# Gate projections of branches A and D for two token groups: computed in the groups' first phase and stored, instead of beside the scan

## The chip, the core and the metric

The kernel runs on one core of one Trainium2 chip. The metric is the device time of one execution in microseconds (us), the median of several runs. Engines: PE is TensorE (matmuls; PEld is its loading of weights), DVE is VectorE, ACT is ScalarE, POOL is GpSimd, SP issues the DMAs. Each engine works through its own instructions in order and waits for others by semaphores.

## What is computed

One layer of a hybrid backbone over two sets of tokens (2048 latent tokens and 128 context tokens, 1024 channels). What matters here of the reference:

```
h = rmsnorm(x, norm_g) * (1 + scale[:, None]) + shift[:, None]
p = h @ w_in
qkv, g_a, beta_logit, a_logit, uv, g_b, x_c, g_c, x_d, g_d = jnp.split(p, _split_points(), axis=-1)
y_a, S_new = deltanet_branch(qkv, g_a, beta_logit, a_logit, S0, ...)   # short conv, chunked scan, both directions
y_b = sgu_branch(uv, g_b, ...)
y_c = pool_branch(x_c, g_c, pool_w, pool_scale)
y_d = fourier_branch(x_d, g_d, fourier_w)
out = jnp.concatenate([y_a, y_b, y_c, y_d], axis=-1) @ w_out
return x + gate[:, None] * out, S_new
```

Every branch ends in a product with `silu(g)` of its own gate columns, 256 columns of `p` each. `g_a` and `g_d` depend on `h` alone: they can be computed at any time at which `h` is in memory.

## The kernel before

The 2176 tokens are cut into three groups: 0 and 1 have 768 tokens each (12 chunks of 64), group 2 has 640, with the context tokens. The two operands of a projection are each held as a pair of fp32r parts (hi and lo) and multiplied in three matmuls (`mm3`, L250), over 8 slices of the channels: 24 matmuls for one tile of output in PSUM. `BIG` holds the group's normalized tokens `hT` for one group at a time, and beside it a ring of three slots for weights. `load_w` (L236 to L243) fetches a weight tile of 128 columns in two halves by SP, and splits it: hi by ACT (by DVE when `Ring.late` is set, after the first phase), lo by DVE for the first half and by POOL for the second. `proj_cm` runs such projections in chunks of tokens, into PSUM tiles `pj` of which there are three.

**The first phase**, `phase_a(gi)` for the groups 0, 1, 2 in turn: `x_fin` writes the group's `hT`; then come the columns of branch D and the decay inputs (`in_wxd`), branch C (`branch_c`), and for each of two pairs of heads K, then Q and V: `conv_proj` projects and evicts into `raw` (L813), `conv_post` makes the short convolution on DVE (`acc`, L830 and L832) and Silu (L834), squares Q and sums it (L843, L844), `k_tok`, `v_tok` and `pair_pre` write the scan's records to DRAM (`rec_d`, `com_d`). The tiles `acc` and `raw` have two buffers each; V's result stays in its `acc` until `v_tok` has read it. The triangular inverses of a group are solved in `lanes_solve` (L728, L730, a chain of steps shared by DVE and POOL) and written by `lanes_out` (L752 to L788): group 0's beside group 1's first phase, those of groups 1 and 2 together after it. Work of group 2's later projections (`r_store`, `r_gate`, `r_b`) runs beside that solve.

**The scan** (`scan`, L1043 to L1072) takes 34 steps, 2 for the context and 32 for the latent tokens, forward and backward at once. A step is a chain: matmuls with the state S, two operations on DVE (L1054, L1055), matmuls, a copy on ACT (`xn`, L1061), matmuls, and the new state on DVE (L1065). Its operands `R` and `C` are loaded by SP for each step (L1032, L1034), two steps deep. Between its steps PE runs the rest of the projections: for group 1 and then for group 0, `r_load` brings `hT` back from DRAM (`h_d`), `r_b` computes branch B, `r_gate(gi, 0)` the gate and product of branch C; `fourier` runs between r_b(1) and r_gate(1, 0). Gate A is `r_store(gi, 14, ga_d)`: projected in three chunks of 256 tokens, Silu, stored in DRAM. Gate D is `r_gate(gi, 1)`: projected the same way and multiplied at once with the stored result `raw_d`. For group 2 both were computed and stored (`ga_d`, `gd_d`) before the scan.

**The output** follows in 17 tiles of 128 tokens, the context first, then from the middle outwards (7, 8, 6, 9, ...): tile 7 and tile 8 need 18 steps of the latent scan, and each further pair two more. One tile is 96 matmuls of 256 columns (`yh`, `yl`), and its weights `wos` replace `hT` in `BIG`, so no output matmul can run before the last projection.

A scheduler orders each engine's instructions when the program is built: by priority, in the order of the code, where an instruction that isn't ready by its own account of time lets later ones pass. The engines then run that order.

## Time and profile before

| | us |
|---|---|
| median of 3 runs | 1256.94 |
| lowest, highest | 1252.34, 1257.28 |
| profiled execution, time | 1259.96 |
| profiled execution, span from first to last instruction | 1258.2 |
| granted TensorE clock, mean over the span | 0.917 |

The profile is of one execution. Its time is 1.8 us over its span and 3.0 us over the median. Busy time of an engine is the time in which it has an instruction under way; the granted clock is the share of full speed at which PE was allowed to run, and has two levels, 1.2 and 2.4 GHz, so a mean of 0.63 is a mixture of them. Times in the timelines are from the start of the span.

### The profile page before, as it was taken

The page shows a single profiled execution, that of the slowest core. Times are in us where ns is not written, and L with a number is a line of the kernel's source. Part 1 is how long each engine was busy: PE and PEld are TensorE (multiplying, and loading weights), DVE is VectorE, ACT ScalarE, POOL GpSimd, SP SyncE. Part 2 cuts the span into 40 slices and gives each one's busy share as a digit, 9 for nine tenths or more (in the row PEclk, how much of TensorE's full clock was granted, in tenths as well). Part 3 has the DMA queues.
Part 4 walks back from the last instruction along what each step waited for, and adds up shares of the span by engine and source line. Part 5 has one row for each costly group of instructions (what it writes and reads, how often), then busy time and mean ns, then how long its engine had stood idle before and what let it go on. Part 6 is the DMA issues. An engine that isn't in the chain of part 4 may idle for free.

```text
span 1258.2 us, 28860 instructions
## 1 busy us (share of the span) xinstructions
PE 1100.5 (87%) x11635; PEld 998.4 (79%) x11635; DVE 875.8 (70%) x1864; ACT 414.3 (33%) x836; POOL 560.2 (45%) x551
## 2 busy tenths in 40 slices
PE   5798999986578899878997989999899979999997
PEld 2598888875566889774886878888889969999997
DVE  3768886999987477999577263584433378888665
ACT  2355765444344585310523102112111211111111
POOL 1347456799973154797040033223132543432212
PEclk9999988998766899798998989999999969999999
DMA  9978559543271558425245656767735555544331
GB/s 303 331 265 269 148 136 254 189 102 72 60 169 40 128 129 188 111 82 189 61 122 164 168 149 180 232 211 253 208 119 177 176 169 164 174 144 140 122 126 68
DMA packets 251388, 204.21 MB, mean 162 GB/s; under 512 B 109138, under 2 KB 218706, under 8 KB 250998
## 3 DMA queue, kind: packets, MB, share of 16 engines
q1 hardware_dynamic: 251254, 202.37, 55.1%
q8 instruction: 91, 1.49, 0.5%
q14 instruction: 43, 0.35, 0.1%
HBM read 138.86 MB, written 63.46 MB: 161 GB/s over the span
## 4 chain that ended last, share of the span: by engine, by line
PE 35%; DVE 8%; DMA 7%; POOL 5%; issue 3%; SPq 2%; ACT 1%; DVEq 0%; POOLq 0%; ACTq 0%
PE pj L250 28%; DMA wst<-in_wt_dram 3%; PE pa L1043 3%; POOL LL L730 2%; POOL ltmp L728 2%; DVE BIG L240 1%; DMA tab<-in_cdft_dram 1%; DVE X L752 1%; POOL BIG L243 1%; PE pb L1384 1%; PE pc L1043 1%; SPq L1034 1%; DMA ga<-ga_d 1%; DMA wos<-in_wo_dram 1%; DVE BIG L1207 1%
## 5 line engine op out<-in xcount | busy, mean ns | idle before, releaser
L250 PE MATMUL pj<-BIG 128*128 128x256 f32 (+4 forms) x3888 | 638.6, 320 | 34.0 <-DVE BIG L240 7.8
L250 PEld LDWEIGHTS pj<-BIG 128*128 128x128 f32 x3888 | 581.2, 201 | 54.9 <-issue 13.9
L250 PE MATMUL pj<-BIG,yh 128*128 128x256 f32 x1088 | 196.9, 287 | 5.7 <-ACT BIG L1346 4.7
L250 PEld LDWEIGHTS pj<-BIG,yh 128*128 128x128 f32 x1088 | 164.8, 191 | 8.8 <-ACT BIG L1346 5.1
L243 POOL TENSOR_TENSOR BIG<-wst,BIG 128x512 fp32r<-128x512 f32 (+1 forms) x66 | 94.7, 1436 | 171.9 <-DVE BIG L240 77.7
L250 PE MATMUL pj<-BIG,yl 128*128 128x256 f32 x544 | 141.9, 286 | 0.0
L250 PEld LDWEIGHTS pj<-BIG,yl 128*128 128x128 f32 x544 | 99.0, 191 | 0.7
L240 DVE CAST BIG<-wst 128x512 fp32r<-128x512 f32 (+2 forms) x72 | 44.9, 624 | 75.9 <-DMA wst<-in_wt_dram 41.5
L1404 POOL TENSOR_TENSOR z<-z,xs 128x1024 f32<-128x1024 f32 x16 | 40.2, 2510 | 72.5 <-DVE z L1396 62.0
L832 DVE SCALAR_TENSOR_TENSOR acc<-raw,prm,acc 128x768 f32<-128x768 f32 (+1 forms) x72 | 68.6, 976 | 4.8 <-ACT acc L830 4.8
L1050 POOL TENSOR_TENSOR gS<-S,sc_s 128x256 f32<-128x256 f32 x32 | 21.5, 672 | 97.3 <-DVE S L1065 85.4
L728 POOL TENSOR_TENSOR ltmp<-LL 64x60 f32<-64x60 f32 (+29 forms) x60 | 60.9, 1015 | 5.4 <-ACT LL L717 2.0
L730 POOL TENSOR_TENSOR LL<-LL,ltmp 64x60 f32<-64x60 f32 (+29 forms) x60 | 61.8, 1031 | 3.3
L1365 ACT ACTIVATE yh<-yt 128x768 fp32r<-128x768 f32 (+1 forms) x34 | 20.6, 628 | 125.2 <-issue 59.9
L243 DVE TENSOR_TENSOR BIG<-wst,BIG 128x512 fp32r<-128x512 f32 (+1 forms) x66 | 52.7, 799 | 10.7 <-ACT BIG L242 8.4
L354 POOL TENSOR_TENSOR BIG<-h,BIG 128x384 fp32r<-128x384 f32 (+2 forms) x28 | 32.7, 1167 | 61.6 <-DVE BIG L353 57.8
L730 DVE TENSOR_TENSOR LL<-LL,ltmp 64x60 f32<-64x60 f32 (+29 forms) x60 | 53.8, 896 | 1.1
L242 ACT ACTIVATE BIG<-wst 128x512 fp32r<-128x512 f32 (+1 forms) x60 | 37.6, 633 | 51.1 <-DMA wst<-in_wt_dram 29.4
L728 DVE TENSOR_TENSOR ltmp<-LL 64x60 f32<-64x60 f32 (+29 forms) x60 | 53.2, 887 | 1.3
L1061 ACT ACTIVATE xn<-pa 128x256 f32<-128x256 f32 x34 | 13.0, 381 | 106.9 <-PE pa L1043 106.9
L1212 ACT ACTIVATE g<-pj 128x256 f32<-128x256 f32 (+1 forms) x64 | 22.6, 398 | 70.5 <-PE pj L250 61.3
L1396 DVE TENSOR_TENSOR z<-pj,gbc 128x256 f32<-128x256 f32 x68 | 26.1, 421 | 28.2 <-PE pj L250 27.9
(292 smaller groups left out, 1921.9 us busy)
## 6 DMA issues: line engine op xcount, KB each, us to landing
wst<-in_wt_dram SPq DMA_DIRECT2D x96, 256.0 KB
R<-rec_d SPq DMA_DIRECT2D x136, 128.0 KB
ada<-in_ada_dram SPq DMA_DIRECT2D x24, 512.0 KB
C<-com_d SPq DMA_DIRECT2D x68, 128.0 KB
xs<-xs_d SPq DMA_DIRECT2D x16, 512.0 KB
out_dram<-z SPq DMA_DIRECT2D x16, 512.0 KB
x<-in_xs_dram SPq DMA_DIRECT2D x13, 512.0 KB
xs_d<-x SPq DMA_DIRECT2D x13, 512.0 KB
```

What stands on the lines that cost most here:

```text
L240: nc.vector.tensor_copy(hi[:, ks, a:a + w], st[:, :, :w])
L242: nc.scalar.activation(hi[:, ks, a:a + w], st[:, :, :w], AF.Copy)
L243: (nc.vector if k0 == 0 else nc.gpsimd).tensor_tensor(lo[:, ks, a:a + w], st[:, :, :w], hi[:, ks, a:a + w].bitcast(F32), op=ALU.subtract)
L250: nc.tensor.matmul(out, lh[a](k), rh[b](k), start=(k == first and i == 0), stop=(k == last and i == 2))
L354: (nc.gpsimd if f % 2 else nc.vector).tensor_tensor(hT[1][:, f, off:off + w], h, hi.bitcast(F32), op=ALU.subtract)
L728: eng.tensor_tensor(tv, X[:, bs, j, j + 1:32].unsqueeze(2).to_broadcast([n, nb, j, ni]), bc(X[:, bs, 0:j, j], ni), op=ALU.mult)
L730: eng.tensor_tensor(X[:, bs, 0:j, j + 1:32], X[:, bs, 0:j, j + 1:32], tv, op=ALU.add)
L832: nc.vector.scalar_tensor_tensor(o, raw[:, si + j:si + j + n], w[:, j:j + 1], o, op0=ALU.mult, op1=ALU.add)
L1043: nc.tensor.matmul(ps[o, q], lh(q)[hp], rh[hp, q])
L1212: [lambda a, w, ps, t=t: nc.scalar.activation(t[:, a:a + w], ps[:, :w], func) for t in ts])
L1396: nc.vector.tensor_tensor(z[:, ns], ps, gbc[:, cd, ns], op=ALU.mult)
L1404: nc.gpsimd.tensor_tensor(z, z, xs, op=ALU.add)
```

## The change

For groups 0 and 1 a new function `early_gate` projects two gate tiles in the group's first phase, in two chunks of 384 tokens, behind Q and V of each pair: gate A (tiles 14, 15) in pair 0 and gate D (12, 13) in pair 1. The Silu goes into a tile of tag `acc`, the one that the convolutions use, and is stored in `ga_d` or `gd_d`. Beside the scan, `r_store` for groups 1 and 0 and `r_gate(gi, 1)` go away; the product of branch D is now made for all three groups in one loop at the end, with gate D loaded from `gd_d`.

```diff
+    def early_gate(gi, ct, dst):
+        for m in range(2):
+            t = cv_.tile([128, 784], F32, tag="acc", name="eg")
+            proj_cm([io["wt"][ct + m]], [(0, 384), (384, 384)],
+                    [lambda a, w, ps, t=t: nc.scalar.activation(t[:, a:a + w], ps[:, :w], AF.Silu)])
+            nc.sync.dma_start(out=dst[m, :, 768 * gi:768 * gi + 768], in_=t[:, :768])
+
     def conv_proj(g, cts, chunks):
...
             sv = conv_post(g, 3 * pair + 2, rv, ntok)
             pull()
+            if gi < 2:
+                early_gate(gi, 14 - 2 * pair, (ga_d, gd_d)[pair])
...
     r_gate(1, 0)
-    r_store(1, 14, ga_d)
-    r_gate(1, 1)
     f_es.close()
     op = [ctx.enter_context(tc.tile_pool(name="opa_", bufs=1, side="right", reuse_waits="tile"))]
     r_load(0)
     r_b(0)
     r_gate(0, 0)
-    r_gate(0, 1)
-    for m in range(2):
-        g = gt_(2)
-        nc.sync.dma_start(out=g, in_=gd_d[m, :, tks(2)])
-        r_mul(2, 1, m, g)
-    r_store(0, 14, ga_d)
+    for gi in (1, 2, 0):
+        for m in range(2):
+            g = gt_(gi)
+            nc.sync.dma_start(out=g, in_=gd_d[m, :, tks(gi)])
+            r_mul(gi, 1, m, g)
```

The built order shows the following. On ACT in group 0, behind the last eviction of V of pair 0 (acc_1266 is Q's buffer there, acc_1305 V's, raw_1540 K of pair 1), before:

```order
L834 ACTIVATE sl_1271<-acc_1266 128x768
L813 ACTIVATE raw_1540<-pj_1550 128x384
L813 ACTIVATE raw_1540<-pj_1576 128x392
L681 ACT_TABLE_LOAD
L681 ACTIVATE Pf_1425<-Pf_1425 128x1536
L843 ACTIVATE acc_1266<-pb_1274 128x2x256
L834 ACT_TABLE_LOAD
L834 ACTIVATE acc_1305<-acc_1305 128x768
L843 ACTIVATE acc_1266<-pb_1280 128x2x128
```

and now (eg_1311 and eg_1373 are the two output tiles of gate A; K of pair 1 comes later still):

```order
L841 ACTIVATE sl_1271<-acc_1266 128x768
L681 ACT_TABLE_LOAD
L681 ACTIVATE Pf_1549<-Pf_1549 128x1536
L850 ACTIVATE acc_1266<-pb_1274 128x2x256
L850 ACTIVATE acc_1266<-pb_1280 128x2x128
L841 ACT_TABLE_LOAD
L841 ACTIVATE acc_1305<-acc_1305 128x768
L242 ACTIVATE BIG_90<-wst_1781 128x4x128
L800 ACTIVATE eg_1311<-pj_1320 128x384
L800 ACTIVATE eg_1311<-pj_1346 128x384
```

The eviction of K stood ahead of Q's squares (L843, now L850) and V's Silu; the evictions of gate A stand behind both, and K behind them.

On DVE at the end of group 0's solve (L728, L730; the first output copies of `lanes_out` are L752), before, in group 2's first phase (lg_4030 is its `in_wxd` projection):

```order
L730 TENSOR_TENSOR LL_2297<-LL_2297,ltmp_3293 64x2x30
L610 TENSOR_TENSOR tm_3213<-tm_3213,v1_3238 128x768
L924 COPY lg_4030<-pj_4047 128x16
L924 COPY lg_4030<-pj_4075 128x16
L353 CAST BIG_90<-h_3940 128x128
L752 COPY X2_3537<-LL_2297 48x256
L752 COPY X2_3541<-LL_2297 48x256
```

and now (wst_3687 and wst_4213 are weights of V of pair 1 and of gate D, in group 1):

```order
L243 TENSOR_TENSOR BIG_90<-wst_3687,BIG_90 128x4x128
L670 TENSOR_TENSOR Ld_2803<-Pd_3361,pb_3374 128x192
L670 TENSOR_TENSOR Ld_2803<-Pd_3361,pb_3399 128x192
L670 TENSOR_TENSOR Ld_2803<-Pd_3361,pb_3374 128x192
L670 TENSOR_TENSOR Ld_2803<-Pd_3361,pb_3399 128x192
L676 TENSOR_TENSOR Po_3362<-Po_3362,pb_3374 128x192
L676 TENSOR_TENSOR Po_3362<-Po_3362,pb_3399 128x192
L243 TENSOR_TENSOR BIG_90<-wst_4213,BIG_90 128x4x128
L692 TENSOR_TENSOR Pf_3363<-Pf_3363,pb_3446 128x384 x2
L692 TENSOR_TENSOR Pf_3363<-Pf_3363,pb_3461 128x384 x2
L752 COPY X2_3909<-LL_2545 48x256
L752 COPY X2_3913<-LL_2545 48x256
```

`lanes_out` of group 0 began behind group 2's projection, and now begins inside group 1, behind a solve that ends ahead of V's weights of pair 1.

On ACT at the start of the output (xn is the copy of each scan step, g an eviction of a gate, wos the output's weights, yh its operand), before:

```order
L1061 ACTIVATE xn<-pa 128x256
L1212 ACTIVATE g<-pj 128x256
L1346 ACTIVATE BIG<-wos 128x4x256
L1212 ACTIVATE g<-pj 128x256
L1346 ACTIVATE BIG<-wos 128x4x256
L1212 ACTIVATE g<-pj 128x256
L1061 ACTIVATE xn<-pa 128x256
L1346 ACTIVATE BIG<-wos 128x4x256 x2
L1365 ACTIVATE yh<-yt 128x768
L1061 ACTIVATE xn<-pa 128x256
```

and now:

```order
L1070 ACTIVATE xn<-pa 128x256
L1352 ACTIVATE BIG<-wos 128x4x256
L1070 ACTIVATE xn<-pa 128x256 x2
L1371 ACTIVATE yh<-yt 128x768 x2
L1411 ACTIVATE xs,fs<-z 128x1024
L1070 ACTIVATE xn<-pa 128x256 x4
L1371 ACTIVATE yh<-yt 128x256
```

Between the copies of neighbouring steps stood evictions of gates and output weights; now up to four copies stand side by side with nothing between them.

## Rows read from the trace of the kernel before

**Rows 1.** The page: busy time of each engine, and the granted clock in 40 slices of the span (tenths of full speed).

```profile
PE 1100.5 (87%) x11635; PEld 998.4 (79%) x11635; DVE 875.8 (70%) x1864; ACT 414.3 (33%) x836; POOL 560.2 (45%) x551
...
PEclk9999988998766899798998989999999969999999
```

**Rows 2.** The stages: from and to, length, then busy us (and number of instructions) of PE, PEld, DVE, ACT and POOL, the granted clock, the busy share of the DMA engines, GB/s.

```profile
138.00:182.00 44.00, 40.29 (x355) 36.26 (x353) 38.45 (x63) 28.65 (x41) 25.24 (x25) 0.92 0.47 116
...
276.00:346.00 70.00, 43.37 (x347) 39.75 (x347) 69.72 (x80) 32.47 (x50) 67.30 (x50) 0.81 0.27 63
346.00:416.00 70.00, 57.84 (x418) 48.55 (x415) 53.05 (x126) 31.91 (x72) 35.20 (x47) 0.63 0.47 105
...
600.00:711.00 111.00, 93.63 (x1362) 86.73 (x1362) 66.65 (x151) 38.32 (x117) 19.65 (x14) 0.91 0.43 120
...
711.00:1001.00 290.00, 272.46 (x3464) 247.88 (x3453) 136.72 (x310) 50.28 (x124) 86.65 (x70) 0.97 0.63 189
1001.00:1043.00 42.00, 31.68 (x441) 28.62 (x440) 31.74 (x101) 7.87 (x13) 20.17 (x20) 0.76 0.58 170
1043.00:1133.00 90.00, 89.89 (x1303) 84.84 (x1303) 76.54 (x230) 17.28 (x32) 35.78 (x36) 1.00 0.54 166
1133.00:1259.00 126.00, 116.94 (x1101) 114.98 (x1099) 84.76 (x247) 22.43 (x44) 29.68 (x22) 0.98 0.33 114
```

**Rows 3.** Timelines of PE at four places: start, duration of the row, and the count of matmuls in it. In order: a run in group 0's first phase, the first matmul of the scan, a run of gate A of group 0 beside the scan, and the last matmul of the kernel.

```profile
141.96 5.21 PE L250 MATMUL pj<-BIG 128*128 128x392 f32 x28
...
710.68 0.27 PE L1043 MATMUL pa<-S,C 64*64 64x64 f32 x1
...
996.44 2.62 PE L250 MATMUL pj<-BIG 128*128 128x256 f32 x20
...
1249.66 0.28 PE L250 MATMUL pj<-BIG,yl 128*128 128x256 f32 x1
```

**Rows 4.** Groups of instructions by line: count, busy us, mean ns of one, idle us of the engine before them. The preparation of weights (L242, L243), the eviction of gates and its table load (L1212), the product with a gate (L1234).

```profile
L243 POOL TENSOR_TENSOR BIG<-wst,BIG 128x512 fp32r<-128x512 f32 (+1 forms) x66 | 94.7, 1436 | 171.9 <-DVE BIG L240 77.7 <-ACT BIG L242 33.5 <-PE pj L250 30.5
...
L243 DVE TENSOR_TENSOR BIG<-wst,BIG 128x512 fp32r<-128x512 f32 (+1 forms) x66 | 52.7, 799 | 10.7 <-ACT BIG L242 8.4 <-PE pj L250 0.5
...
L242 ACT ACTIVATE BIG<-wst 128x512 fp32r<-128x512 f32 (+1 forms) x60 | 37.6, 633 | 51.1 <-DMA wst<-in_wt_dram 29.4 <-DMA wst<-in_wxd_dram 11.8 <-PE pj L250 8.5
...
L1234 POOL TENSOR_TENSOR rw<-rw,g 128x768 f32<-128x768 f32 (+1 forms) x12 | 23.4, 1958 | 20.5 <-DMA rw<-raw_d 20.5
...
L1212 ACT ACTIVATE g<-pj 128x256 f32<-128x256 f32 (+1 forms) x64 | 22.6, 398 | 70.5 <-PE pj L250 61.3 <-POOL rw L1234 9.0
...
L1212 ACT ACT_TABLE_LOAD x5 | 6.4, 1283 | 11.2 <-PE pj L250 10.7 <-issue 0.4
```

**Rows 5.** Waits of SP's queue from 80 to 650 us: the waiting line and who ended the wait, us in total, times, the longest. L238 are the loads of weights.

```profile
SPq L238 <- POOL BIG L243: 84.0, 29, 10.8
```

**Rows 6.** Timeline of ACT in group 0, from the last eviction of V of pair 0: that eviction, the eviction of K of pair 1 (two), V's Silu, and the second half of Q's squares.

```profile
141.68 0.48 ACT L813 ACTIVATE raw<-pj 128x392 f32<-128x392 f32 x1
...
149.43 0.86 ACT L813 ACTIVATE raw<-pj 128x384 f32<-128x384 f32 x2
...
155.65 0.84 ACT L834 ACTIVATE acc<-acc 128x768 f32<-128x768 f32 x1
156.40 0.36 ACT L843 ACTIVATE acc<-pb 128x256 f32<-128x256 f32 x1
```

**Rows 7.** The same place in group 1, on ACT: an eviction of Q as PE ends V, the eviction of K of pair 1 (two), and V's Silu.

```profile
276.16 0.48 ACT L813 ACTIVATE raw<-pj 128x392 f32<-128x392 f32 x1
...
301.28 0.86 ACT L813 ACTIVATE raw<-pj 128x384 f32<-128x384 f32 x2
...
308.99 0.85 ACT L834 ACTIVATE acc<-acc 128x768 f32<-128x768 f32 x1
```

**Rows 8.** The updates of the solve on DVE (L730) in stretches of the first phase: from and to, length, busy us and count, granted clock, DMA share, GB/s.

```profile
228.00:276.00 48.00, 7.94 (x13) 0.93 0.51 132
276.00:336.00 60.00, 12.94 (x11) 0.83 0.26 58
336.00:368.00 32.00, 4.19 (x8) 0.71 0.60 141
```

**Rows 9.** The steps of the scan: the copy `xn` on ACT (L1061), one for each step, counted in the stretches of the scan; columns as in rows 8.

```profile
711.00:1001.00 290.00, 8.41 (x22) 0.97 0.63 189
1001.00:1043.00 42.00, 1.14 (x3) 0.76 0.58 170
1043.00:1133.00 90.00, 3.04 (x8) 1.00 0.54 166
```

**Rows 10.** Timeline of one step: a new state on DVE (L1065), a subtraction for the output's weights (L1347), the next state; and SP's issues of the loads for a step.

```profile
999.81 0.42 DVE L1065 TENSOR_TENSOR S<-pa,gS 128x256 f32<-128x256 f32 x1 [3.93 <-PE pc L1043]
...
1000.67 2.38 SPq L1032 DMA_DIRECT2D R<-rec_d  x4
...
1001.22 2.30 DVE L1347 TENSOR_TENSOR BIG<-wos,BIG 128x1024 fp32r<-128x1024 f32 x1 [0.65 <-ACT BIG L1346]
...
1003.15 1.00 SPq L1034 DMA_DIRECT2D C<-com_d  x2
...
1007.43 0.42 DVE L1065 TENSOR_TENSOR S<-pa,gS 128x256 f32<-128x256 f32 x1 [2.46 <-PE pc L1043]
```

**Rows 11.** Waits from 997 to 1045 us, the longest in total: who waited for whom, us in total, times, the longest.

```profile
ACT BIG L1346 <- DMA wos<-in_wo_dram: 12.0, 3, 6.8
```

## The prediction

> **What bounds the kernel now.** I read the shares and the clock line of the page first, then the stages, then single timelines, then the steps of the scan. TensorE (PE) is busy for 87% of the span, and its granted clock falls in the middle of the first phase [rows 1]. The stages say where PE is the limit [rows 2]. From 711 to 1001 us, where the scan runs with projections between its steps, PE is busy 272 of 290 us at a clock of 0.97, and from 1043 us on it is full: whatever matmul goes away there shortens the kernel, as long as the scan does not become the limit. In the first phase it is different. From 276 to 346 us PE is busy 43 of 70 us at 0.81, while VectorE (DVE) has 69.7 and GpSimd (POOL) 67.3 of the 70; from 346 to 416 us PE is busy 58 us at 0.63. Busy time times granted clock is 35 and 36 us of full-speed work: 69 of these 140 us of PE are lost. In group 0 (138 to 182 us) the same sum leaves 7 of 44 us.
>
> **What is removed.** Gate tiles A and D of groups 0 and 1: 8 tiles of 72 matmuls of 256 columns. A run of 20 of them takes 2.62 us, its last one 0.28, so 0.123 us each [rows 3]; 576 x 0.123 = 71 us, all in the PE-bound stretch. With them go 8 weight preparations, two halves each, on DVE and POOL [rows 4], which are not full there.
>
> **What is added.** The same 8 tiles as 48 matmuls of 384 columns each, in the first phase. A run of 28 of 384 and 392 columns takes 5.21 us there, about 0.18 each [rows 3]: 8.7 us per tile, 69 us in all. The wider chunks neither cost nor save. The Trainium skill ("Perfetto Trace Analysis", Matmuls) holds that larger matmuls are more efficient, and "TensorE: Matmul & The Clock Gate" (Back-to-back issue gap) gives 81 ns at 128 columns and 131 at 512; an estimate from these two is 0.114 us at 384, 44 us for the eight tiles and a result 25 us lower than mine, to which I give no chance, since the rows here have 0.46 to 0.48 ns a column at either width. The weights bring one subtraction per tile to DVE (0.80 us) and one to POOL (1.44), 6.4 and 11.5 us, half of it where both are full; two copies (0.63) and two Silu evictions (0.4) per tile on ACT, and 12 table loads more in the program (1.28) [rows 4], are hidden, since ACT is busy 32 us of the 70 where it is needed most [rows 2]. The products with gate D (1.96 us on POOL [rows 4]) only move. SP issues 8 stores of gates in the first phase instead of 4 later, and 4 loads of gate D more beside the output. A store waits for its eviction with weight loads behind it on SP; those wait there anyway for the preparations, 84 us behind POOL alone [rows 5], so I add nothing. If that cover were gone, the next weights would be late by the length of the eviction's wait, which is priced next.
>
> **What the gates wait for.** A gate's output tile takes one of the two "acc" buffers, which the convolutions of Q and V hold. So its eviction stands on ACT behind Q's squares and V's Silu, and K1's behind that, as the order shows. In group 0 V's last projection is evicted at 141.7 us, V's Silu and Q's squares end at 156.5 and 156.8, and K1 is evicted at 149.4 [rows 6]. PE can run 72 of gate A's 96 matmuls (13 us) in the meantime and then idles some 6 us. In group 1 PE is done with V at 276, V's Silu ends at 309.8, and K1 is evicted at 301.3 [rows 7]: now K1 must follow 310 by the rest of gate A and its own 8.7 us, so its eviction comes near 321, 20 us later. For group 0 I take +34: 35 us of tiles, 12 of waits, and 13 back, because DVE does the pair's convolutions and its later steps while PE does gates, and K1 to V1 then wait less for them. For group 1 I take +20 for gate A and +18 for gate D (13 of matmuls and a shorter wait), and give back half of the 69 us that PE loses from 276 to 416, 35 us: the solve of group 0 goes on beside the gates (the order has it done by V1's weights, where 8 of its 32 DVE updates stood after 336 us [rows 8]), the step behind it moves up, and the stretch from 138 to 182 us, in which PE is busy for 92%, is granted 0.92, not 0.63 [rows 2]. **The first phase grows by G = 34 + 38 - 35 = 37 us.** The ends are far apart: with all of it given back, held only by DVE, which is full from 276 to 346 us and starts that stretch some 15 us later, G is 15; with nothing given back it is 72. I take the middle: PE runs in order and can't fill every hole, but from 346 to 416 us DVE is not full (53 of 70), and it is the clock that is low.
>
> **Where the removed time goes.** The scan keeps its 34 steps; I counted in the two programs' orders what stands between them. Before the first output matmul there were 22 steps with 1478 projection matmuls, and now there are 13.3 steps with 839. A step took 290 / 22 = 13.2 us [rows 9] with 67 matmuls beside it; now it has 63: 13.3 x 13.2 = 176 us. Then 7.7 steps have only 147 output matmuls between them, because output tiles 7 and 8 need step 19. No row shows a bare step. The three from 1001 to 1043 us, with few matmuls but the preparation of the output weights, took 14 us each at a clock of 0.76 [rows 2, 9]. In the first of them, from one state's end on DVE at 1000.2 us to the next's at 1007.9, the chain takes 7.6 us, some 2 of them behind a weight subtraction on DVE, and the loads for a step are 2.4 + 1.0 us of SP [rows 10], no bound at that pace. I take 8 us a step, 60 in all, nearer to the chain than to the loaded steps; the ends are 6 us (45) and the 11.2 of a step beside output work (84). Steps 21 to 33 run beside output tiles as before, 13 x 90 / 8 = 146 us [rows 9]. Behind the last step stand 6.25 output tiles instead of 9.4: the end took 125 us from 1133, 8 of them after the last matmul at 1249.9 [rows 2, 3], so 117 / 9.4 = 12.4 us a tile, 78 + 8 = 86 us. From the scan's start that is 176 + 60 + 146 + 86 = 468 us, against 547 (710.7 to 1258.2) [rows 3]. Ahead of it stand 63 more matmuls of group 1's B gate, 7.7 us, half of it in holes (PE is busy 94 of 111 us there [rows 2]): 4 us.
>
> **Sum.** 711 + 37 + 4 + 468 = 1220 us of span. The profiled run was 1259.96 us with a span of 1258.2, and 3 us over the median, so **1219 us**, 3% less.
>
> **The rivals.**
> (a) *More comes back in the first phase*: G = 15, with the gates beside the solve. For it: the 69 lost microseconds. Against it: half of the gates lie in group 0, where PE has 7 to spare. 1197 us.
> (b) *The scan becomes the limit*: steps without filler take the 11.2 us of those beside output work, because the loads of the output's tiles and weights share the queue with the state's; ACT waited 12.0 us for the output weights at that place already [rows 11]. 84 instead of 60: 1243 us.
> (c) *The first phase pays in full, and more*: each gate pair holds PE until V's Silu, since its output tile has no buffer of its own, and nothing comes back. With G = 72 the time is 1254; with a wait of 19 us for each pair of group 1 (72 matmuls from 276 end near 291, the Silu at 310 [rows 7]) G is 110 and the time 1292. The change is slower from G = 81 on. The Trainium skill ("Perfetto Trace Analysis", Identifying the Most-Contended Engine) reads a gap that repeats as a sign that the next tile finds no buffer; this would be such a gap, four times. Against it: the DVE work that is waited for has to be done anyway, and is done earlier.
>
> **How the numbers follow.** The forecast (1205 to 1235) has 0.49, (a) 0.14, (b) 0.13, (c) 0.24. Within 0.5% of the median (1251 to 1263), about what a measurement can tell from no change, lie 0.10 of (c); slower are 0.14 of it; faster is the rest, 0.76. The range, 1194 to 1254, holds (a), (b) and the mildest part of (c).
>
> **What would show it.** Right: the scan's first matmul near 752 us instead of 711; a granted clock over 0.8 from 320 to 450 us; the solve's updates of group 0 all ahead of V1's eviction; K1 of group 1 evicted some 55 us later than 301, with part of that gone again by the start of the scan; seven or eight steps of 6 to 9 us with PE near idle; and the last step 86 us before the end. Wrong: a scan start beyond 790 us (c), bare steps of 11 us and more (b), or holes of PE behind gate evictions with DVE idle as well.

## The result, and the profile after

The changed kernel takes 1262.88 us (median of 20 runs, 1252.52 to 1270.87), the kernel before 1252.18 in 20 runs beside it; the ratio is 1.0085, 95% interval 1.0062 to 1.0109 (one of the 20 runs of before took 1655.6 us and is left out of the ratio). So the change makes the kernel slower by 0.9%, where 3% less was forecast, and the time lies outside the range. The profiled execution of after took 1262.04 us, with a span of 1260.3; it lies 0.8 us below its kernel's median. The profiled execution of before (1259.96) lies 7.8 us above the median of these 20 runs.

The page of after, as [rows 1] of before: PE has 4 us less to do, DVE 22 less, and the granted clock is a little higher before the scan (0.91 against 0.88 in the first rows of the stages below).

```profile
PE 1096.1 (87%) x11443; PEld 992.8 (79%) x11443; DVE 853.8 (68%) x1848; ACT 441.8 (35%) x856; POOL 552.5 (44%) x551
...
PEclk9898998989789769899899899998998789999999
```

The stages of after, cut at the first matmul of the scan, at its steps 13, 21 and 33 (counted by the copy xn from 0), and at the end; columns as in [rows 2].

```profile
0.00:763.00 763.00, 655.57 (x5792) 588.06 (x5793) 543.35 (x990) 353.15 (x672) 388.67 (x414) 0.91 0.56 158
763.00:964.00 201.00, 175.88 (x2143) 155.75 (x2144) 115.93 (x239) 37.42 (x88) 58.13 (x43) 0.96 0.64 193
964.00:1037.00 73.00, 50.92 (x834) 45.53 (x834) 33.05 (x90) 9.74 (x18) 27.87 (x24) 0.77 0.74 226
1037.00:1174.00 137.00, 135.75 (x1944) 126.91 (x1943) 105.08 (x371) 26.22 (x49) 57.06 (x55) 1.00 0.52 162
1174.00:1260.00 86.00, 78.02 (x738) 76.54 (x737) 56.37 (x159) 15.28 (x31) 20.78 (x16) 0.98 0.30 107
```

The kernel before, cut at the same events (its steps 13 and 21 are at 904 and 997 us, its step 33 at 1133):

```profile
0.00:711.00 711.00, 589.56 (x5345) 522.11 (x5345) 545.99 (x977) 316.48 (x624) 387.90 (x404) 0.88 0.57 159
711.00:904.00 193.00, 178.96 (x2164) 160.73 (x2153) 105.63 (x244) 33.28 (x86) 52.84 (x42) 0.96 0.70 209
904.00:997.00 93.00, 89.50 (x1244) 83.56 (x1243) 30.33 (x64) 14.64 (x34) 32.85 (x28) 1.00 0.50 152
997.00:1133.00 136.00, 125.56 (x1800) 117.04 (x1798) 109.04 (x332) 27.52 (x48) 56.91 (x56) 0.92 0.55 166
```

Read the two as a balance of PE's busy and idle time. The first phase is 52 us longer: 66 us more of busy time, and only 14 less of idle (107 instead of 121). The scan part is 497 us instead of 547, so 50 shorter: 71 us of matmuls are gone (512 to 441 busy), but 21 us of new idle time stand there (36 to 57). In these two executions 52 against 50 leaves 2 us. The medians differ by 10.7 us, because the profiled execution of before was longer than the median; one trace does not show where these 8 us lie. The medians of e1 below put the late gates at 47 us and the early ones at 57. Most of the new idle time lies in steps 13 to 20, where PE is busy 51 of 73 us at a clock of 0.77; before it was 89.5 of 93. Steps 0 to 13 did not get shorter at all, 201 us instead of 193.

The bare steps, by the copy xn on ACT (L1070, L1061 before) in steps 17 to 21 of after; in brackets ACT's idle time ahead of it, and what ended it:

```profile
1011.04 0.39 ACT L1070 ACTIVATE xn<-pa 128x256 f32<-128x256 f32 x1 [3.70 <-PE pa L1052]
1017.76 0.38 ACT L1070 ACTIVATE xn<-pa 128x256 f32<-128x256 f32 x1 [6.33 <-PE pa L1052]
1021.94 0.38 ACT L1070 ACTIVATE xn<-pa 128x256 f32<-128x256 f32 x1 [3.80 <-PE pa L1052]
1026.57 0.38 ACT L1070 ACTIVATE xn<-pa 128x256 f32<-128x256 f32 x1 [4.24 <-PE pa L1052]
...
1036.85 0.39 ACT L1070 ACTIVATE xn<-pa 128x256 f32<-128x256 f32 x1 [5.08 <-PE pa L1052]
```

A step with next to nothing on PE beside it can take 4.2 us (1017.76 to 1021.94). The eight of them took 73 us and are not alike: 4.2 to 14.7 us, with PE busy for 51 of the 73. In that stretch (964 to 1037 us) ACT waited for the output's weights and for its operand, in us in total, times, the longest:

```profile
ACT BIG L1352 <- DMA wos<-in_wo_dram: 15.0, 4, 7.6
...
ACT yh L1371 <- DMA yt<-y_d: 7.9, 2, 4.4
```

How much of the 73 us these waits hold, no run shows.

The place of [rows 6] after the change, on ACT in group 0: V's Silu, the two evictions of the first gate tile that PE had ready at 152, one of the second, and K's two.

```profile
155.94 0.84 ACT L841 ACTIVATE acc<-acc 128x768 f32<-128x768 f32 x1
...
157.21 0.85 ACT L800 ACTIVATE eg<-pj 128x384 f32<-128x384 f32 x2
...
168.90 0.49 ACT L800 ACTIVATE eg<-pj 128x384 f32<-128x384 f32 x1
...
176.65 0.49 ACT L820 ACTIVATE raw<-pj 128x384 f32<-128x384 f32 x1 [4.65 <-PE pj L250]
...
177.56 0.49 ACT L820 ACTIVATE raw<-pj 128x392 f32<-128x392 f32 x1
```

K of pair 1 is evicted at 177 us instead of 149.

### The profile page after: what moved, and what is told of

It is laid out like the page before. It is cut to its first block, busy times and chain, and to the rows that moved or that the text cites. A ratio compares the mean times of both kernels' runs of the same rounds, so it can differ in the third digit from the quotient of the medians.

```text
span 1260.3 us, 28495 instructions
## 1 busy us (share of the span) xinstructions
PE 1096.1 (87%) x11443; PEld 992.8 (79%) x11443; DVE 853.8 (68%) x1848; ACT 441.8 (35%) x856; POOL 552.5 (44%) x551
## 4 chain that ended last, share of the span: by engine, by line
PE 44%; DVE 24%; DMA 11%; issue 7%; ACT 5%; POOL 3%; SPq 2%; DVEq 0%; ACTq 0%; POOLq 0%
PE pj L250 32%; DVE ltmp L728 3%; DVE acc L839 2%; PE pa L1052 2%; DVE LL L730 2%; DMA wst<-in_wt_dram 2%; DMA tab<-in_cdft_dram 1%; DVE BIG L240 1%; DVE BIG L243 1%; PE pc L342 1%; DVE rt L311 1%; DMA rec_d<-XF 1%; PE pb L1291 1%; DVE acc L886 1%; DVE BIG L1216 1%
## 5 line engine op out<-in xcount | busy, mean ns | idle before, releaser
L250 PE MATMUL pj<-BIG 128*128 128x256 f32 (+4 forms) x3696 | 622.1, 324 | 25.4 <-ACT raw L820 6.7
L250 PEld LDWEIGHTS pj<-BIG 128*128 128x128 f32 x3696 | 569.7, 198 | 46.2 <-issue 11.9
L243 POOL TENSOR_TENSOR BIG<-wst,BIG 128x512 fp32r<-128x512 f32 (+1 forms) x66 | 94.1, 1426 | 165.3 <-DVE BIG L240 72.0
L243 DVE TENSOR_TENSOR BIG<-wst,BIG 128x512 fp32r<-128x512 f32 (+1 forms) x66 | 54.2, 821 | 32.0 <-ACT BIG L242 30.7
L730 POOL TENSOR_TENSOR LL<-LL,ltmp 64x60 f32<-64x60 f32 (+29 forms) x60 | 63.3, 1055 | 3.7
L1371 ACT ACTIVATE yh<-yt 128x256 fp32r<-128x256 f32 (+1 forms) x34 | 21.1, 632 | 119.6 <-PE pj L250 43.5
L242 ACT ACTIVATE BIG<-wst 128x512 fp32r<-128x512 f32 (+1 forms) x76 | 47.6, 632 | 43.3 <-DMA wst<-in_wt_dram 19.0
L354 POOL TENSOR_TENSOR BIG<-h,BIG 128x384 fp32r<-128x384 f32 (+2 forms) x28 | 26.4, 944 | 79.7 <-DVE BIG L353 75.9
L728 DVE TENSOR_TENSOR ltmp<-LL 64x60 f32<-64x60 f32 (+29 forms) x60 | 57.9, 965 | 1.6
L1372 DVE TENSOR_TENSOR yl<-yt,yh 128x256 fp32r<-128x256 f32 (+1 forms) x34 | 43.9, 1305 | 18.1 <-ACT yh L1371 18.0
L728 POOL TENSOR_TENSOR ltmp<-LL 64x60 f32<-64x60 f32 (+29 forms) x60 | 52.4, 873 | 6.7 <-ACT LL L717 3.6
L240 DVE CAST BIG<-wst 128x512 fp32r<-128x512 f32 (+2 forms) x56 | 33.9, 610 | 29.1 <-PE pj L250 13.0
L1070 ACT ACTIVATE xn<-pa 128x256 f32<-128x256 f32 x34 | 13.1, 384 | 101.5 <-PE pa L1052 101.2
L353 DVE CAST BIG<-h 128x384 fp32r<-128x384 f32 (+2 forms) x56 | 26.8, 485 | 31.4 <-ACT h L344 31.4
L730 DVE TENSOR_TENSOR LL<-LL,ltmp 64x60 f32<-64x60 f32 (+29 forms) x60 | 47.0, 784 | 1.3
```

Of the source, the lines that this page charges most:

```text
L240: nc.vector.tensor_copy(hi[:, ks, a:a + w], st[:, :, :w])
L242: nc.scalar.activation(hi[:, ks, a:a + w], st[:, :, :w], AF.Copy)
L243: (nc.vector if k0 == 0 else nc.gpsimd).tensor_tensor(lo[:, ks, a:a + w], st[:, :, :w], hi[:, ks, a:a + w].bitcast(F32), op=ALU.subtract)
L250: nc.tensor.matmul(out, lh[a](k), rh[b](k), start=(k == first and i == 0), stop=(k == last and i == 2))
L353: nc.vector.tensor_copy(hi, h)
L354: (nc.gpsimd if f % 2 else nc.vector).tensor_tensor(hT[1][:, f, off:off + w], h, hi.bitcast(F32), op=ALU.subtract)
```

## The experiments

Each was timed beside the kernel before on the same chip; the ratio is to it (changed kernel: 1.0085). "Start" is the scan's first matmul in the profiled run, "scan part" runs from there to the end of the span. Before has 711 and 547, after 763 and 497. Start and scan part come from one execution of each kernel, and that execution can lie 6 to 8 us off the median (before itself, e5 and e12 do), so differences of that size between two of them say little; the ratios are the firmer figures.

| run | us | ratio, 95% interval | start | scan part |
|---|---|---|---|---|
| e1 no gates | 1206.5 | 0.963 (0.960 to 0.966) | 712 | 493 |
| e2 three pairs early | 1270.8 | 1.015 (1.011 to 1.018) | 755 | 514 |
| e3 one pair early | 1268.4 | 1.011 (1.008 to 1.014) | 716 | 552 |
| e4 group 0 early | 1276.9 | 1.018 (1.015 to 1.021) | 745 | 528 |
| e5 third of the matmuls | 1263.5 | 1.005 (1.002 to 1.009) | 770 | 498 |
| e6 products sooner | 1291.3 | 1.027 (1.024 to 1.031) | 759 | 527 |
| e7 gate D early | 1265.7 | 1.008 (1.005 to 1.011) | 730 | 534 |
| e8 Fourier sooner | 1284.4 | 1.022 (1.019 to 1.025) | 715 | 567 |
| e9 no eviction | 1251.8 | 0.998 (0.995 to 1.001) | 756 | 493 |
| e10 all behind V1 | 1261.9 | 1.007 (1.004 to 1.010) | 761 | 493 |
| e11 A behind K1 | 1260.8 | 1.005 (1.002 to 1.008) | 762 | 497 |
| e12 no products | 1256.5 | 1.002 (0.999 to 1.005) | 757 | 492 |
| e13 no weights | 1263.1 | 1.008 (1.005 to 1.010) | 772 | 493 |
| e14 weights only | 1220.1 | 0.973 (0.971 to 0.975) | 725 | 494 |
| e15 third, no eviction | 1227.4 | 0.981 (0.978 to 0.985) | 726 | 497 |
| e16 all behind V0 | 1271.3 | 1.016 (1.012 to 1.019) | 768 | 503 |
| e17 spread | 1252.6 | 1.000 (0.998 to 1.002) | 758 | 492 |
| e18 group 1 early | 1246.4 | 0.995 (0.991 to 0.998) | 727 | 515 |

### What each side is worth

e1 takes the gates out of both places:

```diff
-            t = cv_.tile([128, 784], F32, tag="acc", name="eg")
-            proj_cm([io["wt"][ct + m]], ...)
-            nc.sync.dma_start(out=dst[m, ...], in_=t[:, :768])
+            nc.sync.dma_start(out=dst[m, ...], in_=rv[:, :768])
```

> The changed kernel without the work of the eight gate tiles: neither early nor late are they projected; the first phase stores the convolution input of V in their place, so the transfers stay. It prices both sides by themselves. My theory (the trace after): the early gates cost the first phase 52 us and the late ones were worth 51 beside the scan, since about 20 of their 71 us of matmuls only covered holes that are now open; so about 1205 us, the scan's first matmul near 711 and steps 13 to 20 with PE idle as in the changed kernel. Rival (the scan was no longer bound by PE, and the late gates were hidden for the most part): 1230 us or more.

1206.5 us, as the trace had said: the late gates were worth 3.7% of the kernel before (some 47 us), not 71, and the early ones cost all of that and some 10 us more. Its first phase and its bare steps (13 to 20, the last row):

```profile
0.00:712.00 712.00, 591.31 (x5349) 523.96 (x5349) 542.53 (x976) 315.57 (x625) 382.72 (x404) 0.88 0.57 163
712.00:903.00 191.00, 177.59 (x2168) 158.65 (x2158) 101.41 (x245) 37.26 (x87) 56.11 (x43) 0.96 0.67 203
903.00:981.00 78.00, 53.60 (x883) 47.91 (x882) 34.07 (x91) 11.77 (x21) 30.72 (x25) 0.82 0.73 218
```

The first phase is that of before, and the scan part has the open steps of after (493 us against 497): the two sides add up, to within a few us.

### Which of the gates

The list of pairs that are early is changed (`if gi < 2` becomes a list), and the others get their late calls back.

```diff
-            if gi < 2:
+            if (gi, pair) in ((0, 0), (1, 0), (1, 1)):      # e2
+            if (gi, pair) in ((1, 1),):                     # e3
+            if (gi, pair) in ((0, 0), (0, 1)):              # e4
+            if (gi, pair) in ((0, 1), (1, 1)):              # e7
+            if (gi, pair) in ((1, 0), (1, 1)):              # e18
```

> Gate D of group 0 is computed late, beside the scan, as before; the other three pairs of gates stay early. My theory: the pairs differ by place; in the trace after, V of group 1 comes 38 us later because of gate D of group 0 alone (the matmuls of the two gates of pair 0 cost 13 each, those of gate D of group 1 nothing). So the first phase shrinks by 25 to 38 us, the scan's first matmul comes at 725 to 738, and the late pair (17.5 us of matmuls) goes into steps that are nearly bare: 1225 to 1240 us, faster than both kernels. Rival (every pair costs about the same, 13 us early and 13 late): 1258 to 1263 us.

> Only gate D of group 1 is computed early; the other three pairs are late as before. My theory: in the trace after it cost nothing between the end of V1 and the end of group 2's first projections, so the scan begins 0 to 5 us later than in the kernel before, and 17 us of matmuls are gone from a stretch that PE bounds: 1232 to 1242 us. Rival (equal pairs): 1250 to 1256 us.

> Gates A and D of group 0 early, those of group 1 late. My theory: 13 + 36 us more ahead of group 1, of which up to 10 come back before the scan, and 35 us less beside it: 1255 to 1270 us, as slow as the change as a whole. Rival (equal pairs): 1252 to 1258 us.

> Gate D of both groups early, in pair 1; gate A of both late. From the starts of the scan in the runs so far (5 us later with gate D of group 1 alone, 45 with three pairs, 52 with all four, 35 with both of group 0) the pairs cost about 25 us each behind pair 0 and 5 to 10 behind pair 1; so the scan begins 14 to 18 us later than in the kernel before, at 725 to 729. The scan part lost about 20 us of cover in each of these runs however many pairs were taken out, so it is 530 to 535 us long: 1256 to 1264 us. Rival (equal pairs): the scan begins at 737 and is 522 long, about 1260 us as well; the start of the scan tells them apart.

For e2 and e3 both sides missed: these kernels are slower than either forecast. The starts went as read from the trace for e3 (5 us later) and nearly so for e7 (19, where 14 to 18 was expected; its time, 1265.7, is just above its range), less so for e4 (34, where 39 to 49 was expected) and e2 (45, where 14 to 27 was). What failed is the scan part: with one pair gone from it (17.7 us of matmuls) it was 5 us longer, with two pairs 20 (e4) and 14 (e7) shorter, with three 33 and with four 50. A pair's late gates have no price of their own. e4 came out above its range for this reason, in spite of its earlier start. e18 was made last, when it was known that place within a group gives nothing:

> Gates A and D of group 1 early, those of group 0 late. In the traces the stretch from V of pair 0 of group 0 to that of group 1 grew by 51 us with all four pairs early, and the stretch from there to the end of group 2's first projections by 13; with group 0's gates alone early the scan began 35 us later. If the two groups differ, as these say, the scan begins 12 to 22 us later than in the kernel before, at 723 to 733, its part is about 528 us as in the run with group 0's gates early, and the time is 1250 to 1262 us. Rival (a pair costs 13 wherever it stands): the scan begins at 737 or later and the time is 1262 us or more.

Start 727, as expected, and the scan part is 515 us, 13 less than expected; 1246.4 us, below its range, and faster than the kernel before and than the changed one. The interval lies clear of 1, though the gain of 0.5% is about the least that can be told. Its stages, cut as above:

```profile
0.00:727.00 727.00, 613.15 (x5582) 549.70 (x5582) 538.31 (x983) 338.67 (x653) 385.98 (x409) 0.91 0.57 160
727.00:930.00 203.00, 182.99 (x2184) 163.00 (x2183) 112.55 (x249) 34.76 (x86) 59.77 (x46) 0.94 0.65 194
930.00:1016.00 86.00, 75.83 (x1084) 69.49 (x1082) 39.68 (x93) 18.00 (x34) 32.26 (x27) 0.96 0.69 208
1016.00:1154.00 138.00, 135.98 (x1944) 127.02 (x1945) 109.96 (x368) 25.59 (x48) 55.68 (x55) 1.00 0.52 162
1154.00:1242.00 88.00, 79.38 (x760) 77.75 (x756) 57.34 (x164) 15.63 (x32) 20.79 (x16) 0.98 0.31 108
```

Steps 13 to 20 still have work (76 of 86 us at 0.96, against 51 of 73 at 0.77). With e4 it divides the result by group: group 0 pays 34 us ahead of the scan and gets 20 back, group 1 pays 16 and gets 33. Both sums, 50 and 53, are about those of the whole change, 52 and 50.

### What the early gates cost in the first phase

Four edits of `early_gate` take its parts away: two of the three products (e5), the eviction (e9), the weights (e13), all but the weights (e14), and in e15 two products and the eviction.

```diff
+        P = ((0, 0), (0, 1), (1, 0))[:1 if Ring.thin else 3]           # e5, e15: in mm3
-        [lambda a, w, ps, t=t: nc.scalar.activation(t[:, a:a + w], ...)])
+        [lambda a, w, ps: None])                                       # e9, e15
-        proj_cm([io["wt"][ct + m]], ...)
+        proj_cm(None, ...)               # e13: the weights of V, still in the ring
+        load_w(io["wt"][ct + m], 128)    # e14: in place of proj_cm
```

> The changed kernel with one of the three products of the hi and lo parts in the early gates: 8 matmuls for an output tile instead of 24, while weights, preparations, evictions, stores and their places stay (so the gates are computed at lower precision). It tells the matmuls from the waits in the first phase's 52 us. If PE's time is what the early gates cost, two thirds of their 67 us go, 45: the scan's first matmul comes at 718 to 730 and the time is 1216 to 1230 us. Rival (the evictions' place behind V's Silu, the preparation of the weights): PE waits instead, the scan begins at 745 or later and the time is 1245 us or more.

> The changed kernel whose early gates are projected in full, but not evicted: no Silu, no output tile; the store takes the convolution input of V in their place, so the gates are left out of the result. Matmuls and weights stay, the wait of the evictions behind V's Silu goes. With a third of the matmuls the first phase was as long as with all, so something else than PE's time holds it. My theory now: two chains run side by side there, the matmuls (17 us for a pair of tiles, ahead of K of pair 1) and the eviction's wait behind V's Silu, and each alone is nearly long enough; without the wait the scan's first matmul comes at 735 to 750 instead of 763 and the time is 1238 to 1250 us. Rival 1 (the wait is all): at 725 or earlier, 1228 us or less. Rival 2 (the weights' preparation and queue are what costs): at 755 or later, 1255 us or more.

> The changed kernel whose early gates take the weights of V, which lie in the ring already, instead of loading and preparing their own (so they are not the gates' values): matmuls, evictions and stores stay, the load, the hi part and the lo part of eight weight tiles go. In the runs with a third of the matmuls and without evictions the scan began at 770 and 756 us, about where it does with all of them (763), and without any of it at 712. Theory W: what all of those runs share is the weights, a chain of load, ACT, VectorE and GpSimd that each tile goes through in order; then the scan begins at 730 or earlier and the time is 1230 us or less. Theory P: the place is what costs, and any one of matmuls, evictions or weights is enough to hold the next group's tokens, which can be written only behind the group's last projection; then the scan begins at 750 or later, 1248 us or more.

> The other half: the eight weight tiles are loaded and prepared in the early gates' places, but there are no matmuls and no evictions (the store takes the convolution input of V; the gates are left out). Theory W: the scan begins at 745 or later and the time is 1240 us or more. Theory P: with nothing on PE behind V1, the next group's tokens come as in the kernel before, the scan begins at 712 to 725 and the time is 1207 to 1220 us.

> The changed kernel with a third of the matmuls in the early gates and without their evictions: weights, places and 8 matmuls for an output tile stay (the gates are left out of the result). It separates what theory P leaves open: the length of the two chains, or the place alone. In all runs with four early pairs the next group's tokens (the copy h on ACT, from PE's transposes) begin at 205 to 213 us, in the kernel before at 159 and with weights alone at 171, since they can overwrite the tokens only behind the group's last projection. Place alone (the gates' few matmuls stand on PE behind work that waits for the convolutions of pair 1): h begins at 200 or later, the scan at 745 or later, 1240 us or more. Length (matmuls and evictions are each long enough, and neither is there now): h begins at 171 to 185, the scan at 725 to 737, 1220 to 1232 us.

e5 removed 256 of the 384 early matmuls and gave next to nothing back: its time is about that of after, and its start, 770, is from the longest of its 12 runs, 6 us above their median. ACT and PE of e5 at the place of [rows 6], group 0 (L843 is V's Silu, L802 the gate's eviction, L822 K's):

```profile
158.30 0.84 ACT L843 ACTIVATE acc<-acc 128x768 f32<-128x768 f32 x1
...
162.29 0.87 ACT L802 ACTIVATE eg<-pj 128x384 f32<-128x384 f32 x2
...
179.49 0.48 ACT L822 ACTIVATE raw<-pj 128x392 f32<-128x392 f32 x1
```

```profile
141.98 1.67 PE L252 MATMUL pj<-BIG 128*128 128x384 f32 x8 [0.45 <-ACT raw L822]
...
162.84 4.85 PE L252 MATMUL pj<-BIG 128*128 128x384 f32 x14 [2.52 <-ACT eg L802]
```

PE was through with what the three PSUM tiles hold at 143.7 us, stood (but for small transposes and the like of the convolutions) until ACT evicted the first gate behind V's Silu, and the second half of K came at 179, no sooner than in after. e9 alone gave little as well (start 756, as its second rival has it, and 1251.8 us, 11 us less than after, between its forecast and that rival). The first phases of e5 and e9 show the exchange: e5 has 26 us less of busy time on PE than e9, but 40 more of idle time (143 against 103).

```profile
0.00:770.00 770.00, 626.98 (x5550) 554.69 (x5550) 552.51 (x990) 353.20 (x672) 391.48 (x414) 0.88 0.55 157
0.00:756.00 756.00, 652.73 (x5790) 584.43 (x5790) 545.53 (x990) 332.21 (x646) 375.74 (x414) 0.93 0.56 160
```

e15 takes both away and the start falls to 726:

```profile
0.00:726.00 726.00, 604.84 (x5418) 539.90 (x5418) 549.49 (x984) 324.63 (x635) 391.47 (x412) 0.89 0.58 165
```

The stage of e14, with the weights alone:

```profile
0.00:725.00 725.00, 586.39 (x5369) 514.86 (x5370) 557.82 (x990) 332.92 (x647) 395.26 (x414) 0.89 0.59 166
```

So the weights (with their queue) cost 13 us by themselves (725 against 712 in e1), and the other 38 (763 less 725) belong to two chains beside each other, the matmuls and the evictions' wait, of which each by itself is nearly as long as both: on top of the weights the matmuls without evictions add 31 us (e9), the evictions with a third of the matmuls 45 (e5, in its longest execution), a third of the matmuls alone about 1 (e15; by the ratios e15 takes 0.8% longer than e14). The time and the start of e15 are those of "length"; the next group's tokens began at 191 us, between "length" (171 to 185) and "place" (200 or later), so the place may have a small share. The weights as the one cause (theory W) fell with e13, which left them out and won nothing, and e14.

Other places within the group:

```diff
-            if gi < 2:
-                early_gate(gi, 14 - 2 * pair, (ga_d, gd_d)[pair])
+            early_gate(gi, 14, ga_d); early_gate(gi, 12, gd_d)   # e10: behind V of pair 1; e16: of pair 0
+            early_gate(gi, 14, ga_d)    # e11: behind K of pair 1; gate D stays
+            early_gate(gi, 12, gd_d)    # e17: behind K of pair 1; gate A stays
```

> The changed kernel with both early pairs of a group, gate A and gate D, behind Q and V of pair 1; nothing behind pair 0, so K of pair 1 keeps its place behind V of pair 0. One pair behind V1 cost 5 to 10 us, since PE waits there for the next group's tokens anyway; a second fills what is left of that hole and pays for the rest. The scan's first matmul at 733 to 745, the scan part as in the changed kernel (497): 1232 to 1244 us, faster than both. Rival (the cost of a pair doesn't depend on its place): at 763, 1260 us.

> The changed kernel with gate A behind K of pair 1 instead of ahead of it; gate D stays behind V1. K's eviction then doesn't stand behind the gates', and VectorE gets K's convolution early. Where the place ahead of K1 is what makes gate A dear (25 us a pair), the scan's first matmul comes at 735 to 748 instead of 763 and the time is 1235 to 1248 us. Rival (gate A then holds Q and V of pair 1 as it held K, and nothing is won): 760 or later, 1258 us or more.

> The changed kernel with both early pairs of a group, gate A and gate D, behind Q and V of pair 0; nothing behind V of pair 1, so that the next group's tokens follow V1 as in the kernel before. If the dear place is the one between V1 and the next group's tokens, the cost of a group is the delay of K1 alone, 15 to 25 us: the scan begins at 742 to 755 instead of 763 and the time is 1238 to 1252 us. Rival (the sum of the gates' work is paid wherever it stands): 760 or later, 1258 us or more.

> As the run before, with gate A behind V of pair 0 and gate D behind K of pair 1: again nothing between V1 and the next group's tokens, and the two pairs lie beside two different stretches of VectorE's work. The scan begins at 738 to 752, the time is 1235 to 1250 us. Rival (paid wherever it stands): 760 or later, 1258 us or more.

The starts are 761, 762, 768 and 758: the price is paid wherever the gates stand, as the rivals of e10, e11 and e16 said; e17 lies between its forecast and its rival. In e10 K1 came at 149, as before, and V1 even earlier (175 instead of 183), and the next group's K at 303, as in after. e17 is the best place of these, 1.000 of before.

### What the scan part lost

```diff
     r_gate(1, 0)
+    # e6: the products with gate D of groups 1 and 2 here, not at the end
...
-    r_b(1)
     fourier(fd)
+    r_b(1)      # e8, otherwise as e3
...
-            nc.sync.dma_start(out=raw_d[2 + m], in_=yd)
+            nc.sync.dma_start(out=y_d[6 + m], in_=yd)      # e12, and no products
```

> The changed kernel with the products with gate D of groups 1 and 2 right behind branch C's gate of group 1 instead of at the end; those of group 0 stay last. In the trace after, the chain from 971 to 1005 us, in the nearly bare steps, runs through the loads of these products, their multiplication and the load of an output tile's operand. If that is what the bare steps lose, 10 to 15 us go: 1247 to 1253 us. Rival (the bare steps wait for the output's weights and the scan's own chain): 1257 us or more.

> The kernel with only gate D of group 1 early, with the Fourier branch placed ahead of branch B of group 1 instead of behind it. In that kernel's trace (the scan 5 us longer though 17 us of matmuls were gone from it) steps 8 and 9 of the scan took 22.8 and 20.7 us, with VectorE working on the second half of the Fourier branch and on the reload of the tokens of group 0 at the same time; gate D had kept these two apart. If this collision is the loss, the two steps come back to 11 to 14 us and the time falls from 1268 to 1248 to 1256 us. Rival (the loss isn't tied to the Fourier branch): 1264 us or more.

> The changed kernel without the products with gate D: the Fourier branch's result goes straight to where the output reads it, and the loads of gate D and of that result, the products and their stores are left out. If these transfers hold the nearly bare steps (13 to 20, which take 73 us although two of them need only 4.2 and 4.6), the eight steps take 45 to 55 us and the time is 1238 to 1248 us. Rival (the output's weights and the scan's own loads and chain hold them): 65 us or more, 1255 us or more.

All three theories of a single culprit fell. e6 and e8 are 2 to 3% slower than before: steps of 5 to 10 us now come early (from step 4 on), PE runs out of projections there, and the first output matmul comes only in step 23 and 28. In e12 steps 13 to 20 took 65 us instead of 73: the products' transfers hold them by 8 us at most.

## Why the prediction was wrong, point by point

Its sum against the trace of after:

| term | predicted | measured |
|---|---|---|
| start of the scan (711 + 37 + 4) | 752 | 763.0 |
| 13.3 steps to the first output matmul (961.8) | 176 | 198.8 |
| 7.7 nearly bare steps (to 1026.6) | 60 | 64.8 |
| steps 21 to 33 (to 1173.5) | 146 | 146.9 |
| behind the last step | 86 | 86.8 |
| span | 1220 | 1260.3 |

**What comes back in the first phase.** Two sizes failed here. Group 0 was put at +34, and e4 measured 34. That is in part luck: in e4 the first K of group 1 came 46 us later than in before (306 against 260), and 12 of these came back only after that. Group 1 was put at 38 less 35; e18 measured 16. The step that failed is "give back half of the 69 us": with the 38 as they stand, some 22 came back. But the 38 do not stand either. K1 of group 1 was put 20 us later by gate A alone and came 40 later in e18 (341 against 301): the matmuls that were left behind V's Silu, 24 of gate A and K's 48, are 13 us of work, as the prediction has it, but PE took from 312 to 342 us for them, since it waited in between at small matmuls for the pair's records (L660 at 326.9 and 330.8 us, released by copies on ACT). V1 then came 27 us later, the first K of group 2 14. So both the delay and what comes back of it are larger than the prediction has them; gate D has no figure of its own here. The order had it right that the solve of group 0 ends ahead of V1 (its last update on DVE is at 358 us, V1's last eviction at 400), and the clock did rise, to 0.87 and 0.86 where before has 0.81 and 0.63:

```profile
276.00:346.00 70.00, 53.86 (x281) 52.28 (x281) 69.30 (x100) 26.29 (x45) 58.54 (x39) 0.87 0.36 102
346.00:430.00 84.00, 72.58 (x563) 68.67 (x564) 59.60 (x101) 53.42 (x90) 57.09 (x63) 0.86 0.53 129
```

Part of the low clock stands later now: from 416 to 481 us after was granted 0.75, before 0.95. And K1 of group 1 came at 378 us, 77 later than 301, not 55:

```profile
377.75 0.49 ACT L820 ACTIVATE raw<-pj 128x384 f32<-128x384 f32 x1 [4.94 <-PE pj L250]
```

With one idle figure for the whole phase the size is plain: 14 of 121 us of PE's idle time were filled.

**The steps of the scan.** This is the larger error, 23 of 40 us. The step that failed is the rate of 13.2 us, taken from 22 steps and used for the first 13.3. It was a mean over a stretch that isn't uniform: before, steps 0 to 13 took 193 us (13.8 for each of 14), and those from 13 to 21 took 93 (11.6). The steps that were left bare are the later, shorter ones. That makes about 8 of the 23 us. About as much is the count: by the copies xn the first output matmul came 13.9 steps after the start, not 13.3. The rest is that the first 14 steps grew, to 201 us, with 3 us less of busy time on PE but 11 more of idle time. Most of that is in the Fourier branch, where PE waited 11.5 us in after (from 773 to 964 us) and 3.6 in before (from 722 to 904), for its tables and for DVE. The largest of these waits, in us in total, times, the longest; the first two after, the third before:

```profile
PE pb L1182 <- DVE Z L1121: 5.4, 1, 5.4
PE pb L1184 <- DMA tab<-in_cdft_dram: 5.2, 4, 1.9
...
PE pb L1175 <- DMA tab<-in_cdft_dram: 2.9, 3, 1.8
```

Why they grew stays open. The sum could have been checked: by its own count 639 matmuls leave the scan part (the gates' 71 us and 8 of group 1's B gate, which now run ahead of it), and it shortens that part by just these 79 us. So it lets no idle time open, although it makes nearly eight steps bare; 21 us of it opened. A part that PE bounds can't give back more than the matmuls that leave it, less the idle time that opens.

**What was right.** The price of a matmul in the first phase (39 of gate A's, from 141.63 us on, took 7.13 us, 0.18 each), the bare steps as a whole (65 us, though unlike each other), the tail, and that PE stands at the gates' evictions behind V's Silu (rival (c)'s mechanism, shown by e5). But (c) took that wait as added to the matmuls; e5, e9 and e15 show that it lies beside them. The time, 1262.88 us, is one that (c) covers, but not for its reason: (c) has the first phase longer by 72 us or more, and it grew by 52. The Trainium skill ("Perfetto Trace Analysis", Optimization Strategy, the section behind the one that the prediction names) says that a gap which keeps repeating can mean that there is no buffer for the next tile; the row of e5 agrees, with PE at 162.84 us released by the eviction, and e9 shows that closing the gap alone gives 7 us of the 52. The prediction's estimate from the Trainium skill ("TensorE: Matmul & The Clock Gate", Back-to-back issue gap) would have made the eight tiles 44 us; this case's trace does not agree, since 0.18 us a matmul make them 69. Rival (b) did not come: the bare steps took 8.4 us each by the prediction's count of them, 9.1 by the copies, not 11.2. That the weights add nothing was wrong: e14 has 13 us for them.

**Still open.** Why a single pair taken from the scan gives nothing (e3) while two of group 1 give 33 us (e18): the built order of all engines shifts with each, and no run held it fixed. And why e17's places end 10 us lower than those of after: in the two profiled executions 5 of it are in the start, 5 in the scan part.

## What to carry to other kernels

Before a sum is believed, write it as a balance for the engine that bounds: busy time that leaves, busy time that arrives, idle time that opens and closes; a saving above the busy time that leaves must name the holes that it closes. Judge a move place by place: here the same edit loses in the group whose PE is nearly full (e4) and gains a little in the group with holes (e18), and half of the change is better than all of it. That the holes are the reason is argued from the stages, not tested. When one part of a cost is taken away and nothing happens, take away two: chains side by side hide each other.

## What was not expected of the hardware

A step of the scan's chain, through PE, DVE, ACT and back, can run in 4.2 us; the shortest step in the trace of before, with other work between, took 9.2 (996.6 to 1005.8). And idle time and a low granted clock came together beside the scan: in steps 13 to 20 of after PE is idle for 22 of 73 us, and the mean granted clock there, a mixture of 1.2 and 2.4 GHz, is 0.77; in before, with 3.5 of 93 us idle, it is 1.00. It is not so in every stretch: from 416 to 481 us of after PE is busy for 62 of 65 us, and the granted clock is 0.75. What makes it fall, no run here separates.
